# Down-projection weights of a SwiGLU stage: lower parts made by an accumulating DMA in place of VectorE

## The chip, the cores and the metric

The kernel runs on one core of a Trainium2 chip. The metric is the time of one execution on the device in microseconds (us); the lower, the better. The engines are named as the profile names them: PE is TensorE's matmul side and PEld its weight load, DVE is VectorE, ACT is ScalarE, POOL is GpSimd, and SP is SyncE, whose queue issues most DMAs here ("SPq" in the profile).

## The reference, cut to what matters

Two layers work on 640 token rows (128 of a context, 512 of a latent) of 1024 features. Each layer is SwiGLU, mixer (a convolution with a gating unit in layer 0, attention in layer 1), SwiGLU, each with a norm, a modulation and a gated residual around it. So there are four SwiGLU stages, and the change lies in these alone:

```python
def swiglu(h, wg, wu, wd):
    return (jax.nn.silu(h @ wg) * (h @ wu)) @ wd
...
    xp = residual(xp, swiglu(pre(xp, mp, norm_w[l, 0], 0), *f1), mp, norm_w[l, 1], 0, 0.5)
    xs = residual(xs, swiglu(pre(xs, ms, norm_w[l, 0], 0), *f1), ms, norm_w[l, 1], 0, 0.5)
```

Here `wg` and `wu` are 1024 x 2816 and `wd` is 2816 x 1024, all float32.

## The kernel before

Every large product is made of three. Each operand `w` is held as an upper part `hi` (`w` rounded to float32r) and a lower part `lo = w - hi`, and `mm3` (L198) adds hi·hi, hi·lo and lo·hi in PSUM. So every weight tile that comes from DRAM is split: `wload` (L178) issues the load on SP's queue into a `raw` tile, has ACT copy it to `hi`, and has DVE subtract `hi` from `raw` into `lo`. There are three `raw` buffers and six buffers each for `hi` and `lo`. A `raw` buffer is free for the next load when the last of its readers is done.

TensorE, VectorE and ScalarE execute their instructions in the order in which the program writes them (class `InOrder`, L58), so a copy that waits for its load holds up all that ACT has behind it. SP issues its loads in order too.

`ffn` (L557) works through the 22 chunks of 128 hidden features in four parts, `PARTS = [(0, 5), (5, 10), (10, 16), (16, 22)]`. For each chunk it runs two units, on token columns 0 to 383 (GA) and 384 to 639 (GB): 48 products each, then SiLU on ACT, a multiplication on DVE and a split of the result. At the end of each of the first three parts follow the down-projections of that part, first for output features 0 to 511 (here called half 0), then for 512 to 1023 (half 1): five token tiles, each a group of 15 products (18 in the third part) with a moving operand of 512 columns, taken from `wd`, and added to y. The weights of a half come in three pieces by `wdown` (L591): each holds two chunks (512 KB), but the third piece of the first two parts holds one (256 KB). `wdown(0)` is written ahead of the last chunk's GA unit, `wdown(1)` after the first token tile of half 0. The pieces are called first, second and third below. The fourth part loads its weights otherwise (L601, L632) and is not touched.

In between, `background` (L265) runs the modulation of later stages: a 512 KB load into a `raw` buffer (`mod_chunk`, L495) and two long multiply-and-sum instructions on DVE for each.

Of the kernel before, what the change touches and what calls it, by code (L numbers as in the profile page):

```python
# [18 lines left out]
T = NT * P  # L19
# [9 lines left out]
# the features of an attention head: first halves of both rotated quarters' pairs, then the second halves  # L29
HALVES = np.arange(64).reshape(2, 2, 16).transpose(1, 0, 2).reshape(64)  # L30
PARTS = [(0, 5), (5, 10), (10, 16), (16, 22)]
# token columns: 0..127 context (cond 0), 128..639 latent (cond 1)
# [4 lines left out]
def weave(main, fill, every=3):  # L37
    """run main, with one of fill after each `every` of them, then the rest of fill"""
    fill = list(fill)
    for n, f in enumerate(main):  # L40
        f()
        if n % every == every - 1 and fill:
            fill.pop(0)()
    for f in fill:
        f()


def segs(lo, hi):
    """parts of a token range with one condition: (from, to, condition)"""
    out = []  # L50
    if lo < NP:
        out.append((lo, min(hi, NP), 0))
    if hi > NP:
        out.append((max(lo, NP), hi, 1))
    return out


class InOrder:  # L58
    """an engine whose instructions are issued in the order in which they are written"""
# [18 lines left out]
class Core:  # L78
    """the NeuronCore; tensor, vector and scalar engine in written order"""
# [7 lines left out]
class Builder:  # L87
# [23 lines left out]
    # Slots of a tag are handed out in the order in which their tiles are first written here. Upper and  # L111
    # lower parts come from different engines, so that they have tags of their own.
# [25 lines left out]
    def split(self, src, hi, lo):  # L138
        """src = hi + lo exactly, both with 12 significant bits."""
        self.nc.scalar.activation(out=hi, in_=src, func=AF.Copy)  # L140
        self.nc.vector.tensor_tensor(out=lo, in0=src, in1=hi.bitcast(F32), op=ALU.subtract)

    def table(self, func):
        """has the scalar engine load func's table ahead of its use"""
        self.nc.scalar.activation(out=self.sm(1, "table"), in_=self.ones[:, 0:1], func=func)

    def wload_ahead(self, dram, nblk, blk=P, pieces=1, small=False):
        """starts the load of weights [128, nblk * blk]; closures that split them, and the list of nblk (hi, lo)
        pairs, there after the first of the closures. small: by way of tiles of their own for the pieces"""
# [33 lines left out]

    def fetch(self, key, dram, nblk, blk=P):
        """wload ahead of its use; take() returns it"""
# [3 lines left out]
    def fetch_ahead(self, key, dram, nblk, blk=P):  # L189
        """fetch() with the split left to the two closures that are returned: upper part, lower part"""  # L190
# [7 lines left out]
    def mm3(self, out, w, x, first, last):  # L198
        """out += w^T x with both operands in two parts"""
# [5 lines left out]
    def proj(self, w, h, g):  # L205
        """PSUM [128, n] = w^T h for one 128-wide output chunk, tokens g"""
# [6 lines left out]
    def proj2(self, ws, h, g, inserts=None):  # L213
        """two projections together, feature chunk by feature chunk; inserts: {k: emitted before chunk k}"""
# [9 lines left out]
    def proj_tok(self, ps, h, w, t):  # L224
        """ps [128 tokens of tile t, n] = h^T w"""
# [5 lines left out]
    def rsqrt_ops(self, ssq, scale, engine=None):  # L231
        """1/sqrt(ssq * scale + eps) on a few columns: the result and the instructions. engine: of the iterations"""
# [3 lines left out]
        # v holds -1/2 of the argument, the first guess comes from its bits  # L236
# [34 lines left out]
    def hi_lo(self, src, mods, c, lo, h):  # L271
        """h[c] columns from lo = src * G + shift, split: what makes the upper part and what then makes the lower
        one are to be called"""
# [11 lines left out]
    def turn(self, tiles, c):  # L285
        """PSUM [128 features of chunk c, tokens] from the normalised x"""
# [5 lines left out]
    def tail(self, last, nxt, fetches):  # L292
        """last(t): (closures for the last products of the sub-layer for token tile t, [closures that add the two
        halves to y]). Norms, residual and the next sub-layer's input h follow. What is left of h is in four
        dictionaries: closures to be called before the feature chunks of the next sub-layer's first three units on
        GA and of its first on GB. fetches: closures that start the loads of the next sub-layer's first weights
        and return the two closures that split them."""
# [6 lines left out]
        def sq(t, what, s=None):  # L304
            # sum of squares of x or y
# [13 lines left out]
        def both(tx, ty):  # L319
            # the columns of x[tx] and y[ty] together  # L320
# [64 lines left out]
        # the last tile: what follows its products goes between those of the next sub-layer's first three units  # L385
# [9 lines left out]
        def step(tiles=None, c=None):  # L395
            # transposes of a chunk; upper and lower parts of the one before
# [72 lines left out]
    def last_tail(self, last):  # L469
        """as tail(), for the last sub-layer"""  # L470
# [34 lines left out]
    def mod_final(self, l, slot, what):  # L505
        """what: 0 shift and scale, 1 gate"""
# [16 lines left out]
    def gate_rows(self, l, slot):  # L523
        """gg as rows along the features, the same on every partition"""
# [24 lines left out]
    def glu(self, pg, pu, out, g):  # L549
        """out (hi, lo) columns g = silu(pg) * pu"""  # L550
# [6 lines left out]
    def ffn(self, l, i, h, lead, nxt, fetches, started=None):  # L557
# [29 lines left out]
        for pi, (j0, j1) in enumerate(PARTS):  # L587
# [3 lines left out]
            def wdown(half):  # L591
                return [p for j in range(j0, j1, 2) for m in [min(2, j1 - j)]
                        for p in self.wload(a["wd"][l, i, j:j + m, :, half * 512:half * 512 + 512]
                                            .rearrange("j p m -> p j m"), m, 512)]
# [42 lines left out]
    def last_products(self, xs, ws, xsel=lambda x, t: tuple(u[:, t * P:(t + 1) * P] for u in x)):  # L637
        """for tail(): y[t] += sum over k of xs[k]^T ws[k]"""
# [21 lines left out]
    def conv_gmlp(self, h, lead, nxt, fetches):  # L660
# [46 lines left out]
        def shifted(c):  # L707
            # 32 channels x 4 shifts on the partitions, for the convolution on the tensor engine
# [5 lines left out]
            for q in range(4):  # L714
                nc.gpsimd.memset(sa[q], 0.0)
                for s in range(4):
                    # column j holds position j + s - HALF
# [61 lines left out]
        def mix(c, copy=lambda out, x: nc.scalar.activation(out=out, in_=x, func=AF.Copy)):  # L779
            # position mixing; what follows the products is returned as closures  # L780
# [72 lines left out]
        # LayerNorm over the conv channels, then swish  # L853
# [38 lines left out]
        for n, f in enumerate(parts):  # L892
# [3 lines left out]
            if n == 3:  # L896
                # from here on the products overwrite the normalised channels
# [9 lines left out]
    def first_products(self, dram, xs, xsel=lambda x, t: tuple(u[:, t * P:(t + 1) * P] for u in x), **kw):  # L907
        """y[t] = the first two of the products of an output projection: a function that starts
        the load of one half of the weights (closures that split them), and closures of the products"""
# [19 lines left out]
    def rope(self, s, pos, on_act=False):  # L929
        """s [128, ..]: latent columns, in place, at positions pos; a feature's partner lies 32 partitions off.  # L930
        Closures, and the last of them"""
# [6 lines left out]
        # the sines have the sign that they need with the partner  # L938
# [7 lines left out]
    def attention(self, h, lead, nxt, fetches):  # L946
# [4 lines left out]
        # keys of chunk 8 + n: latent tiles 1 and 2, cached ones, latent tiles 3 and 4, so that those of any window  # L951
        # lie side by side; the prompt's
# [29 lines left out]
        def rope(s, pos, on_act=False):  # L982
            """closures; the sum of each is left until the products of the next"""
# [25 lines left out]
        # upper parts of the keys of one head on both halves of the partitions, lower parts on their own  # L1009
# [48 lines left out]
        # values, tokens on partitions  # L1058
# [7 lines left out]
        def v_tile(t):  # L1066
            """closures: the values of tile t"""
# [8 lines left out]
        # chunk i holds head 8*(i//4) + i%4 in its lower and head 8*(i//4) + 4 + i%4 in its upper half  # L1076
# [3 lines left out]
        def window(t):  # L1080
            """columns of the keys, columns of the mask, values"""
# [6 lines left out]
        def prepare(t, engine=None):  # L1088
            """closures: both parts of the queries of tile t one above the other, upper parts where they were"""
# [554 lines left out]
```

## Time and profile before

| what | value |
|---|---|
| median of 2 runs | 2372.54 us (2371.78 and 2373.3) |
| the profiled execution, first to last instruction (span) | 2369.2 us |
| what lies between the span and the median | 3.3 us |
| DVE busy | 1354.3 us |
| ACT busy | 833.5 us |
| POOL busy | 111.4 us |
| DMA, mean over the span | 108 GB/s |

No time other than the span is given for the profiled execution itself. A profile row names line, engine, operation and tiles ("out<-in"), then the number of such instructions, their busy time and the mean duration of one in ns, and the idle time of the engine just ahead of them with what ended it. Most instructions stand under L68, the helper that records them in order, so groups are told apart by tiles and shapes. DVE's subtraction that makes the lower part of a weight is `w<-raw,w`, ACT's copy that makes the upper part is `w<-raw`. In a timeline row the first number is the start in us from the span's begin, the second the length.

### The profile page before, as it was taken

How to read it: one execution, taken by the hardware profiler on the slowest of the kernel's cores; microseconds unless marked ns; L12 is line 12 of the kernel's file. 1: busy time of each engine (PE TensorE's matmuls, PEld its weight loads, DVE VectorE, ACT ScalarE, POOL GpSimd, SP SyncE). 2: the span in 40 equal slices, each digit the busy share in tenths (PEclk: the TensorE clock that was granted, in tenths of full speed). 3: DMA queues.
4: the chain of work that ended last, by engine and by line, in shares of the span. 5: the costliest groups of instructions: out<-in, count | busy, mean ns of one | idle time of the engine just before them, and what ended most of it. 6: DMA issues, size and time to landing. Idle time of an engine off the chain costs nothing.

```text
span 2369.2 us, 35411 instructions
## 1 busy us (share of the span) xinstructions
PE 2343.9 (99%) x14484; PEld 2147.5 (91%) x14484; DVE 1354.3 (57%) x2419; ACT 833.5 (35%) x1507; POOL 111.4 (5%) x191
## 2 busy tenths in 40 slices
PE   9999999999999999999999999999899999999998
PEld 7999999999789899989899999998866798989897
DVE  5556665668775566523755666656888652333235
ACT  5322222363354221213532212225468553212122
POOL 1000000021100000000100000002220010000000
PEclk9999999999999999999999999999999999999999
DMA  7343444413223444422224444352000222222221
GB/s 290 117 141 134 152 136 163 137 56 101 73 86 98 134 159 131 147 87 90 67 89 139 151 142 160 134 171 75 28 21 17 92 76 85 72 81 81 80 73 70
DMA packets 85026, 256.82 MB, mean 108 GB/s; under 512 B 9824, under 2 KB 11744, under 8 KB 84096
## 3 DMA queue, kind: packets, MB, share of 16 engines
q1 hardware_dynamic: 83984, 252.74, 32.0%
q8 instruction: 113, 1.85, 0.3%
q0 software_dynamic: 880, 1.83, 0.2%
q14 instruction: 49, 0.40, 0.1%
HBM read 248.97 MB, written 2.93 MB: 106 GB/s over the span
## 4 chain that ended last, share of the span: by engine, by line
PE 94%; DVE 3%; POOL 1%; ACT 1%; issue 1%; DMA 1%; SPq 0%; DVEq 0%; POOLq 0%; ACTq 0%
PE ps L68 94%; DVE tmp L68 1%; DVE w L68 1%; DVE Y L68 1%; POOL nwq L68 1%; DVE act L68 0%; DMA X<-x 0%; DVE X L68 0%; DMA act<-wmod 0%; POOL nwy L68 0%; ACT w L68 0%; ACT Y L68 0%; DVE nwy L68 0%; DVE nwq L68 0%; ACT act L68 0%
## 5 line engine op out<-in xcount | busy, mean ns | idle before, releaser
L68 PE MATMUL ps<-act,w 128*128 128x384 f32 (+4 forms) x9984 | 1479.5, 314 | 8.2 <-DVE w L68 6.8
L68 PEld LDWEIGHTS ps<-act,w 128*128 128x128 f32 (+2 forms) x9984 | 1425.0, 186 | 32.8 <-issue 15.8
L68 PE MATMUL ps<-w,act 128*128 128x512 f32 (+1 forms) x3480 | 782.9, 384 | 3.1 <-ACT tmp L68 3.1
L68 PEld LDWEIGHTS ps<-w,act 128*128 128x128 f32 x3480 | 627.4, 189 | 136.3 <-ACT tmp L68 3.5
L68 DVE TENSOR_TENSOR w<-raw,w 128x1024 fp32r<-128x1024 f32 (+1 forms) x313 | 365.1, 1199 | 151.4 <-ACT w L68 149.9
L68 ACT ACTIVATE w<-raw 128x1024 fp32r<-128x1024 f32 (+1 forms) x313 | 315.5, 1030 | 367.5 <-PE ps L68 146.9
L68 DVE CUSTOM_DVE_ANT_0 scr<-raw,cbc 128x1024 bf16<-128x1024 f32 x256 | 312.9, 1222 | 12.0 <-DMA raw<-wmodT 6.9
L68 DVE TENSOR_TENSOR tmp<-tmp,ps 128x384 f32<-128x384 f32 (+1 forms) x176 | 85.7, 487 | 401.2 <-ACT tmp L68 357.1
L68 ACT ACTIVATE tmp<-ps 128x384 f32<-128x384 f32 (+2 forms) x198 | 83.7, 425 | 652.4 <-PE ps L68 652.0
L68 DVE TENSOR_TENSOR act<-tmp,act 128x256 fp32r<-128x256 f32 (+2 forms) x306 | 135.3, 448 | 133.7 <-ACT act L68 132.5
L68 DVE TENSOR_TENSOR Y<-Y,ps 128x512 f32<-128x512 f32 x140 | 95.6, 686 | 192.9 <-PE ps L68 192.7
L68 ACT ACTIVATE act<-tmp 128x256 fp32r<-128x256 f32 (+3 forms) x304 | 128.3, 433 | 124.1 <-DVE tmp L68 123.9
L68 ACT ACTIVATE Y<-ps 128x512 f32<-128x512 f32 (+2 forms) x96 | 50.8, 532 | 147.6 <-PE ps L68 147.1
L68 ACT ACTIVATE tmp<-ps,sh,G 128x256 f32<-128x256 f32 (+1 forms) x120 | 60.3, 525 | 22.7 <-PE ps L68 22.7
L68 ACT ACTIVATE tmp<-Y 128x1024 bf16<-128x1024 f32 (+2 forms) x39 | 35.1, 901 | 71.4 <-DVE Y L68 71.4
L68 DVE SCALAR_TENSOR_TENSOR act<-act,cw,act 128x640 f32<-128x640 f32 (+14 forms) x60 | 54.5, 909 | 1.8
L68 ACT ACTIVATE Y<-X 128x1024 f32<-128x1024 f32 x30 | 31.8, 1059 | 54.3 <-DVE X L68 50.7
L68 PE MATMUL ps<-ident,Y 128*128 128x128 f32 x260 | 46.7, 273 | 2.6 <-DVE Y L68 2.2
L68 DVE CUSTOM_DVE_ANT_0 raw<-ps,ggrow 128x384 f32<-128x384 f32 (+1 forms) x64 | 41.1, 680 | 12.8 <-PE ps L68 11.4
L68 POOL TENSOR_TENSOR nwq<-nwy 128x1 f32<-128x1 f32 (+1 forms) x30 | 17.9, 595 | 613.2 <-DVE nwy L68 611.7
L68 PEld LDWEIGHTS ps<-ident,Y 128*128 128x128 f32 x260 | 34.4, 140 | 11.7 <-DVE Y L68 3.9
L68 ACT ACTIVATE raw<-raw,nmx 128x384 f32<-128x384 f32 (+1 forms) x64 | 42.2, 669 | 1.0 <-DVE nmx L68 0.9
(149 smaller groups left out, 758.6 us busy)
## 6 DMA issues: line engine op xcount, KB each, us to landing
raw<-wmodT SPq DMA_DIRECT2D x128, 512.0 KB, 3.8
raw<-wg SPq DMA_DIRECT2D x88, 512.0 KB, 4.5
raw<-wu SPq DMA_DIRECT2D x88, 512.0 KB, 3.6
raw<-wd SPq DMA_DIRECT2D x80, 512.0 KB, 4.0
act<-wmod SPq DMA_DIRECT2D x24, 256.0 KB, 6.5
ggrow<-grow SPq DMA_DIRECT2D x6, 1024.0 KB, 4.6
raw<-win SPq DMA_DIRECT2D x12, 512.0 KB, 3.7
raw<-wqkv SPq DMA_DIRECT2D x10, 512.0 KB, 3.8
```

The source lines that it names most:

```text
L68: i = method(*args, **kw)
```

## The change

`wdown` calls a new function, `wload_added`, in place of `wload`, for all pieces of the first three parts of each stage. ACT first writes the negated upper part into the `lo` tile (a copy with scale -1), then the upper part into `hi`. Then a DMA on POOL's queue loads the same weights a second time from DRAM and adds them onto `lo`, so that it holds `w - hi`. DVE's subtraction of these pieces is gone. There are 3 pieces x 2 halves x 3 parts x 4 stages = 72 of them. The rest of the diff removes comments, so that later lines have other numbers.

```diff
+    def wload_added(self, dram, nblk, blk):
+
+        n = nblk * blk
+        raw = self.raw(n)
+        cut = lambda u: u.rearrange("p (a b) -> p a b", a=nblk)
+        self.nc.sync.dma_start(out=cut(raw), in_=dram)
+        hi, lo = self.wpair(n)
+        self.nc.scalar.activation(out=lo, in_=raw, func=AF.Copy, scale=-1.0)
+        self.nc.scalar.activation(out=hi, in_=raw, func=AF.Copy)
+        self.nc.gpsimd.dma_start(out=cut(lo), in_=dram, accum_op=ALU.add)
+        return [(hi[:, b * blk:(b + 1) * blk], lo[:, b * blk:(b + 1) * blk]) for b in range(nblk)]
...
             def wdown(half):
                 return [p for j in range(j0, j1, 2) for m in [min(2, j1 - j)]
-                        for p in self.wload(a["wd"][l, i, j:j + m, :, half * 512:half * 512 + 512]
-                                            .rearrange("j p m -> p j m"), m, 512)]
+                        for p in self.wload_added(a["wd"][l, i, j:j + m, :, half * 512:half * 512 + 512]
+                                                  .rearrange("j p m -> p j m"), m, 512)]
```

On ACT, at the first part of the first stage, half 0, these rows stood before (`raw_1060`, `raw_1066` and `raw_1072` are the three pieces as loaded, `ps_1080` is the result of the GA unit that runs meanwhile; a name in brackets after "waits" is a semaphore, DMAHW of a load on SP's queue):

```order
L68 ACTIVATE act_936<-tmp_1049 128x256 [waits DVE_49]
L68 ACTIVATE w_1062<-raw_1060 128x1024 [waits DMAHW5_49]
L68 ACTIVATE w_1068<-raw_1066 128x1024 [waits DMAHW6_49]
L68 ACTIVATE w_1074<-raw_1072 128x512 [waits DMAHW7_49,Activation_49]
L68 ACTIVATE tmp_1130<-ps_1080 128x384 [waits PE_49]
```

In the changed kernel ACT's rows at the same place are these (`raw_1060`, `raw_1067` and `raw_1074` are the pieces, `w_1063`, `w_1070` and `w_1077` their lower tiles):

```order
L68 ACTIVATE act_936<-tmp_1049 128x256 [waits DVE_49]
L68 ACTIVATE w_1063<-raw_1060 128x1024 [waits DMAHW5_49]
L68 ACTIVATE w_1062<-raw_1060 128x1024
L68 ACTIVATE w_1070<-raw_1067 128x1024 [waits DMAHW6_49]
L68 ACTIVATE w_1069<-raw_1067 128x1024
L68 ACTIVATE w_1077<-raw_1074 128x512 [waits DMAHW7_49]
L68 ACTIVATE w_1076<-raw_1074 128x512 [waits Activation_49]
L68 ACTIVATE tmp_1133<-ps_1083 128x384 [waits PE_49]
```

Each piece has two copies on ACT where it had one, the negated one first, and the SiLU of the unit stands behind six copies where it stood behind three.

On POOL's queue the accumulating DMAs follow each other, with the last of the DMAs that set up the convolution ahead of them (DMASW is a semaphore of a DMA on POOL's queue):

```order
L1479 DMA slnb<-slnb 128x4 [waits DMASW2_49]
L193 DMA w_1063<-wd 128x2x512 [waits DVE_49,DMASW3_49,PE_49,Activation_49]
L193 DMA w_1070<-wd 128x2x512 [waits DVE_49,DMASW4_49,PE_49,Activation_49]
L193 DMA w_1077<-wd 128x512 [waits DVE_49,DMASW5_49,PE_49,Activation_49]
L193 DMA w_1225<-wd 128x2x512 [waits DVE_49,DMASW6_49,PE_49,Activation_49]
L193 DMA w_1232<-wd 128x2x512 [waits DVE_49,DMASW7_49,PE_49,Activation_49]
L193 DMA w_1239<-wd 128x512 [waits DVE_49,DMASW0_49,PE_49,Activation_49]
```

All 18 of a stage stand together in this way: no other instruction of POOL stands between those of one stage.

On PE, at the start of the same half 0, the second product and the eighth are the first that need the lower parts of the first and the second piece:

```order
L68 MATMUL ps_1205<-w_1062,act_706 128x512 [waits Activation_49]
L68 MATMUL ps_1205<-w_1063,act_706 128x512 [waits DMASW3_49]
L68 MATMUL ps_1205<-w_1062,act_707 128x512
L68 MATMUL ps_1205<-w_1062,act_708 128x512
L68 MATMUL ps_1205<-w_1063,act_708 128x512
L68 MATMUL ps_1205<-w_1062,act_709 128x512
L68 MATMUL ps_1205<-w_1069,act_800 128x512 [waits Activation_49]
L68 MATMUL ps_1205<-w_1070,act_800 128x512 [waits DMASW4_49]
```

PE's order is as before, but these two products wait for a DMA on POOL's queue where they waited for DVE.

On SP the order of the loads is the same; what they wait for is not, since the `raw` buffers are handed out otherwise. Before:

```order
L159 DMA raw_1060<-wd 128x2x512 [waits DMAHW5_49,DMAHW2_49,DVE_49]
L159 DMA raw_1066<-wd 128x2x512 [waits DMAHW3_49,DVE_49]
L159 DMA raw_1072<-wd 128x512 [waits DMAHW4_49,DVE_49]
L498 DMA raw_1135<-wmodT 128x1024 [waits DMAHW5_49,DVE_49]
L498 DMA raw_1196<-wmodT 128x1024 [waits DMAHW6_49,DVE_49]
```

And now:

```order
L189 DMA raw_1060<-wd 128x2x512 [waits DMAHW5_49,DMAHW2_49,DVE_49]
L189 DMA raw_1067<-wd 128x2x512 [waits DMAHW3_49,DVE_49]
L189 DMA raw_1074<-wd 128x512 [waits DMAHW5_49,Activation_49]
L510 DMA raw_1138<-wmodT 128x1024 [waits DMAHW4_49,DVE_49]
L510 DMA raw_1199<-wmodT 128x1024 [waits DMAHW6_49,Activation_49]
```

The third piece (`raw_1074`) takes the buffer of the first piece as soon as ACT has read it twice; before, it took the buffer of a modulation chunk that DVE had to finish.

## The prediction

> **What bounds the kernel now.** I read the page first: the span, the engines' shares and the chain that ended last.
>
> ```profile
> span 2369.2 us, 35411 instructions
> PE 2343.9 (99%) x14484; PEld 2147.5 (91%) x14484; DVE 1354.3 (57%) x2419; ACT 833.5 (35%) x1507; POOL 111.4 (5%) x191
> ...
> PE 94%; DVE 3%; POOL 1%; ACT 1%; issue 1%; DMA 1%; SPq 0%; DVEq 0%; POOLq 0%; ACTq 0%
> ```
>
> PE is idle for 2369.2 - 2343.9 = 25.3 us, and 94% of the chain is PE. That would not do alone, since matmuls overlap and busy rows can hide a slow pace; so the view by windows over four stretches comes next (the columns are PE, PEld, DVE, ACT and POOL busy, then the granted clock, the DMA share and GB/s): three down-projections, then the stretch of attention.
>
> ```profile
> 105.00:139.50 34.50, 34.50 (x151) 27.94 (x150) 18.67 (x29) 10.11 (x15) 0.00 (x0) 1.00 0.43 145
> 329.40:371.10 41.70, 41.70 (x183) 33.96 (x182) 19.97 (x30) 6.98 (x8) 0.00 (x0) 1.00 0.35 114
> 1969.50:2004.50 35.00, 35.00 (x153) 28.37 (x153) 6.17 (x7) 10.47 (x16) 0.00 (x0) 1.00 0.22 75
> ...
> 1600.00:1800.00 200.00, 188.08 (x1187) 157.93 (x1186) 155.53 (x342) 121.61 (x297) 42.06 (x56) 0.97 0.11 37
> ```
>
> In a down-projection PE has no gap and the full clock, and 34.5 us for 150 products is 0.23 us each. The third row is the test that matters: DVE is busy 6.17 us of 35 there against 18.67 in the first, and PE's pace is the same. About half of PE's idle time, 11.9 us, lies in the stretch of attention. The waits of PE, longest first, and one row of the timeline tell the same:
>
> ```profile
> PE ps L68 <- DVE w L68: 6.8, 2, 6.6
> ...
> 1715.47 0.47 PE L68 MATMUL ps<-act,w 128*128 128x128 f32 x1 [6.57 <-DVE w L68]
> ```
>
> The whole of PE's waiting for DVE's `w` is one wait in attention, whose `w` are query parts and not weights. So DVE's subtraction of down-projection weights delays nothing now.
>
> **The change, part by part.** What goes and what comes is priced by two rows of the view by groups, shapes kept apart:
>
> ```profile
> L68 ACT ACTIVATE w<-raw 128x1024 fp32r<-128x1024 f32 x297 | 305.9, 1052 | 335.9 <-PE ps L68 143.2 <-DMA raw<-wu 76.1 <-DMA raw<-wd 41.1
> ...
> L68 DVE TENSOR_TENSOR w<-raw,w 128x1024 fp32r<-128x1024 f32 x297 | 354.6, 1226 | 144.3 <-ACT w L68 142.8 <-PE ps L68 1.0
> ```
>
> DVE loses 56 subtractions of 1.23 us (512 KB) and 16 of 0.69 us (256 KB, row below), 80 us in all. None of it is on PE's path, so its worth is 0; with all of PE's 25.3 idle us it could not be more than 1.1%. ACT gains 56 copies of 1.05 us and 16 of 0.63 us, 69 us, and goes to some 900 us of 2369: hidden in itself, but the copies move ACT's order, see below. A copy with a scale is taken at the price of the plain one. POOL gains 72 DMA issues:
>
> ```profile
> L1510 POOL DMA_DIRECT2D ggrow<-mask x1 | 0.6, 561 | 0.0
> ```
>
> At 0.56 us each these are 40 us on an engine that is busy for 111, and nothing else of POOL stands between those of one stage, so no Newton step or memset waits behind them.
>
> What decides is when the accumulating DMA has landed and when PE wants its result. First part of the first stage, timeline:
>
> ```profile
> 91.67 2.23 ACT L68 ACTIVATE w<-raw 128x1024 fp32r<-128x1024 f32 x2
> ...
> 97.33 0.63 ACT L68 ACTIVATE w<-raw 128x512 fp32r<-128x512 f32 x1 [3.43 <-DMA raw<-wd]
> 98.00 0.69 DVE L68 TENSOR_TENSOR w<-raw,w 128x512 fp32r<-128x512 f32 x1 [1.09 <-ACT w L68]
> ...
> 104.68 25.68 PE L68 MATMUL ps<-w,act 128*128 128x512 f32 x110
> ...
> 108.84 2.00 ACT L68 ACTIVATE w<-raw 128x1024 fp32r<-128x1024 f32 x2
> ...
> 111.38 0.63 ACT L68 ACTIVATE w<-raw 128x512 fp32r<-128x512 f32 x1 [0.55 <-DMA raw<-wd]
> ```
>
> Half 0 starts at 104.68. Its second product wants the first piece's lower part (104.9), the 8th the second's (106.3), the 14th the third's (107.7). Today all three are there at 98.7, nine us early. Now ACT negates the first piece at 91.67 to 92.72, copies it until 93.77, negates the second until 94.8 and the third, at the latest, until 97.96. That leaves an accumulating DMA 12.2, 11.5 and 9.7 us from its release to PE's need. In half 1, which starts 75 products later at 122.1, the negated copies end at 109.9, 112.0 and 113.7 and the needs are 122.3, 123.7 and 125.1: 12.4, 11.7 and 11.4 us.
>
> The third part has three full pieces and is the tightest:
>
> ```profile
> 307.58 12.20 SPq L159 DMA_DIRECT2D raw<-wd  x3
> ...
> 316.42 1.04 ACT L68 ACTIVATE w<-raw 128x1024 fp32r<-128x1024 f32 x1
> ...
> 317.75 1.06 ACT L68 ACTIVATE w<-raw 128x1024 fp32r<-128x1024 f32 x1 [0.29 <-DMA raw<-wd]
> ...
> 323.18 1.06 ACT L68 ACTIVATE w<-raw 128x1024 fp32r<-128x1024 f32 x1 [4.36 <-DMA raw<-wd]
> ...
> 329.42 41.70 PE L68 MATMUL ps<-w,act 128*128 128x512 f32 x180
> ...
> 330.52 1.04 ACT L68 ACTIVATE w<-raw 128x1024 fp32r<-128x1024 f32 x1
> ```
>
> 41.70 us for 180 products is 0.232 us each. The needs are 329.7, 331.0 and 332.4; the negated copies end at 317.5, 319.6 and 324.2: 12.2, 11.5 and 8.2 us. The last is a lower bound: the third load was issued at 319.4 (the end of the x3 row) and landed 3.8 us later, and it now takes the first piece's buffer, which ACT leaves at 318.5, so about 9 us are left. The SiLU of the unit is then behind six copies and starts near 324.4 to 325.3 where the third copy ended at 324.2; its result is wanted after 15 products of the first tile, at 332.9: hidden. In half 1 (start 350.3) the margins are over 15 us.
>
> Now the DMA. No row of this trace shows an accumulating one. The nearest:
>
> ```profile
> raw<-wd SPq DMA_DIRECT2D x80, 512.0 KB, 4.0
> ...
> raw<-wd SPq DMA_DIRECT2D x16, 256.0 KB, 2.6
> ...
> ggrow<-mask POOLq DMA_DIRECT2D x1, 384.0 KB, 5.0
> ...
> ggrow<-rsin POOLq DMA_DIRECT2D x1, 256.0 KB, 2.9
> ...
> GB/s 290 117 141 134 152 136 163 137 56 101 73 86 98 134 159 131 147 87 90 67 89 139 151 142 160 134 171 75 28 21 17 92 76 85 72 81 81 80 73 70
> ```
>
> From 256 to 512 KB a load grows by 1.4 us, so 512 KB is 1.2 us fixed and 2.8 us of moving; POOL's queue adds 0.3 (2.9 against 2.6). The new DMA reads the weights and also the tile it adds to: twice the bytes read, and I take the moving twice: 1.5 + 5.6 = 7.1 us for 512 KB and 4.3 for 256 KB. The low end is a plain load by POOL, 4.3 us; for the high end I take four times the moving (both reads, the sum and the write one after the other and none overlapped), 12.7 us. I take 7.1 since the load's row is of the same bytes on the same engines. The three of a half can also queue behind each other: their spacing S lies between 5.6 (nothing of two DMAs overlaps) and 3.6 (twice 512 KB at the 290 GB/s that the first slice kept up).
>
> Lateness of the third piece (0 where negative), L being the landing time of 512 KB: half 0 of the first two parts (8 halves) L + 1.5 S - 15.0; half 0 of the third part (4) L + 2 S - 15.0; half 1 of the first part (4) L + 1.5 S - 15.2; the others have 3 to 6 us more. With L = 7.1 and S = 3.6 all are negative: 0. With S = 5.6 they are 0.5, 3.3 and 0.3: 8 x 0.5 + 4 x 3.3 + 4 x 0.3 = 18 us. I take S near 3.6, for the slice held its rate for 59 us. Sum: 0 for DVE, 0 for ACT, 0 for POOL, 0 to 18 for PE's new wait; taken at the low end, the span stays 2369 and the time, 3.3 us above it as in the median of 2372.5, is 2373, with 2369 to 2391 as this case's own range.
>
> The Trainium skill, page "Collectives: The Full Stack", section "The bandwidth ceiling: the fold count and why AG ≠ RS ≠ AR", has a reason for the factor: an add in the DMA path costs its second source read rather than the arithmetic, and it measured 32.35 against 62.28 GB/s for a copy. No run here shows this yet; by that rule the high end of four times would not come about, and the sum would be the one above.
>
> **The rivals.** *Slower: the accumulating DMA becomes PE's wait.* Nothing in the rows excludes a DMA that adds at a third or a quarter of a load's rate, and POOL's queue has an odd row (384 KB in 5.0 us). With L = 1.5 + S the three latenesses reach 47 us in sum (2%) at S = 6.3: 8 x 2.3 + 4 x 5.4 + 4 x 2.1 = 48. That is where it decides. At three times the moving, S = 8.4 and L = 9.9, they are 7.5, 11.7 and 7.3, and the other halves (margins 18.3 and 21.6) 4.2 and 5.1: 60 + 47 + 29 + 17 + 20 = 173, or 2546 us; at four times some 2720. Against it: the margins of 8 to 12 us are two to three plain loads.
>
> *A little slower: the second read takes bandwidth from the loads.* While the first two pieces accumulate, the third is being loaded, then two modulation chunks; the first stages already use a DMA share of 0.35 to 0.43. If one load's moving (512 KB at 290 GB/s, 1.8 us) comes ahead of the accumulating DMAs on the engines, L is 8.9, and with S = 5.6 the latenesses are 2.3, 5.1 and 2.1: 8 x 2.3 + 4 x 5.1 + 4 x 2.1 = 47 us; in the last stage, where no modulation runs (share 0.22), they stay at the 18 / 4 from above, so 0.75 x 47 + 4.5 = 40. The case covers 19 to 47 us, 2391 to 2419. In the Trainium skill, page "DMA: Bandwidth & Descriptors", section "Queues, rings and completion order", each DMA engine takes turns between the queues it has work for, packet by packet, so that a load and an accumulation would each get about half. By that rule this rival holds whenever they meet; no run here shows it.
>
> *Faster: DVE's 80 us come off PE's time.* It would need PE to wait for DVE in these stages; the rows above show no such wait. All of PE's idle time gone gives 2347, still within 2%.
>
> **How the numbers follow.** A change of 2%, 47 us, is about what a measurement of this kernel can tell from none. Likeliest, no wait or up to 18 us: 0.74, predicted time 2373. A little slower, 2391 to 2419: 0.08. Slower by more: 0.16. Faster by more: 0.02. Same is 0.74 + 0.08 = 0.82. The range must hold 8 in 10: from 2366, some us under the likeliest's own 2369 for what runs differ by, to 2415, most of the second case: about 0.81.
>
> **What would show it.** The accumulating DMAs' rows: near 7 us to landing for 512 KB; PE's waits without a row for a DMA into `w`; DVE busy near 1275 us, ACT near 900. Wrong would be PE rows with a gap ahead of the 2nd, 8th or 14th product of a half, longest in the third part: then L or S is mis-sized, and the gap's length says by how much.

## The result, and the profile after

The changed kernel takes 2397.74 us (median of 2 runs, 2396.99 and 2398.49) against 2372.54 before: a ratio of 1.0108, 95% interval 1.0078 to 1.0137. That is 25.2 us more, 1.1%: within the 2% that the prediction calls the same, inside its range of 2366 to 2415, and 24.7 us above the time it named. The size and the place are those of its second case, not of the likeliest one. Of all the executions reported here, two of one kernel ("tile held, in order" in the table below) took 3842 and 6631 us, for no reason that a run shows; its median is that of all nine, its ratio that of the other seven.

The page of the changed kernel, the span, the engines and three groups (instructions, then busy us and mean ns, then idle us ahead of them and what ended most of it):

```profile
span 2396.7 us, 35578 instructions
...
PE 2357.0 (98%) x14484; PEld 2151.6 (90%) x14484; DVE 1280.0 (53%) x2347; ACT 893.1 (37%) x1579; POOL 193.4 (8%) x263
...
L68 PE MATMUL ps<-w,act 128*128 128x512 f32 (+1 forms) x3480 | 794.1, 387 | 17.9 <-DMA w<-wd 14.5
...
L193 POOL DMA_DIRECT2D w<-wd x72 | 81.9, 1140 | 1143.1 <-ACT w L68 1014.7
...
raw<-wd SPq DMA_DIRECT2D x80, 512.0 KB, 4.6
w<-wd POOLq DMA_DIRECT2D x56, 512.0 KB, 10.3
```

VectorE and ScalarE stand where the diff puts them: 74 us less, 60 us more. POOL pays 1.14 us for an issue. The down-projection's products now wait 14.5 us for the adding DMA, which lands 10.3 us after its issue. The waits of PE, which had no such row before (total us, times, longest):

```profile
PEld ps L68 <- DMA w<-wd: 24.7, 24, 2.8
...
PE ps L68 <- DMA w<-wd: 14.5, 17, 2.3
```

Where the time went is read by taking the same PE instruction in both traces, half by half, and asking how much later it starts. Half 0 of the third part loses 4.6, 4.6, 5.7 and 1.3 us in the four down-projections, 16.2 in sum. Half 0 of the first part loses 3.1 in all four, of the second 1.8, half 1 of the first part 4.5, of the second 0.3. These are 25.9 of the 27.5 us between the two profiled spans. Outside the down-projections little is lost: some tenths in attention, and 1.4 us at the start of the program, where some executions run at half the clock for 3.4 us and others do not, with and without adding DMAs.

The tightest place, half 0 of the third part in the first down-projection, in the timeline after (start, length, engine):

```profile
321.63 3.89 ACT L68 ACTIVATE w<-raw 128x1024 fp32r<-128x1024 f32 x4
322.96 1.20 POOL L193 DMA_DIRECT2D w<-wd  x1 [97.77 <-ACT w L68]
323.65 0.37 SPq L189 DMA_DIRECT2D raw<-wd  x1
324.61 1.32 SPq L510 DMA_DIRECT2D raw<-wmodT  x2
324.86 1.20 POOL L193 DMA_DIRECT2D w<-wd  x1 [0.69 <-DVE mf L68]
328.21 2.01 ACT L68 ACTIVATE w<-raw 128x1024 fp32r<-128x1024 f32 x2 [2.69 <-DMA raw<-wd]
329.56 1.19 POOL L193 DMA_DIRECT2D w<-wd  x1 [3.51 <-ACT w L68]
...
334.64 1.78 PE L68 MATMUL ps<-w,act 128*128 128x512 f32 x7
336.62 1.66 PE L68 MATMUL ps<-w,act 128*128 128x512 f32 x6 [0.20 <-DMA w<-wd]
340.59 4.60 PE L68 MATMUL ps<-w,act 128*128 128x512 f32 x12 [2.31 <-DMA w<-wd]
```

The three issues stand at 322.96, 324.86 and 329.56. PE does seven products, waits 0.20 us for the second piece, does six more and waits 2.31 us for the third, which landed 11.0 us after its issue. The third load and a modulation load start between the first and the second issue, a second modulation load 0.7 us after the second. What the 16 DMA engines did from the first issue to the third landing, 17.6 us (digits: tenths busy in 40 slices; queue: packets, MB, share of the 16 engines' time; q0 holds POOL's DMAs, q1 the loads):

```profile
DMA  0009315799999999999999999999999999999999
...
q0 software_dynamic: 816, 1.57, 48.9%
q1 hardware_dynamic: 1061, 2.56, 44.4%
```

From 3.5 us after the first issue every slice is 90% busy or more. 1.57 MB of additions take 0.489 x 17.6 = 8.6 us of all engines, 5.5 us per MB; 2.56 MB of loads take 7.8 us, 3.0 per MB. An addition costs 1.8 times a load here, and while it is under way the loads take nearly as much of the engines as it does. The factor is not a constant: read in the same way in the runs below, from the first issue to the third landing of this half, it is 2.2 or 2.3 (added from the loaded tile; tile held, in order) and 2.5 (added from the tile in rows of 2 KB). The Trainium skill, page "Collectives: The Full Stack", section "The bandwidth ceiling: the fold count and why AG ≠ RS ≠ AR", has two source reads for an add and measured a factor of 1.93. The 1.8 to 2.5 of these runs lie on both sides of it.

The rest of the loss there is the clock (the view by windows: us, busy time of the engines, granted clock, DMA share, GB/s; the three rows are the end of the wait, the 3.5 us after it and what follows):

```profile
335.00:341.20 6.20, 3.69 (x16) 2.38 (x15) 3.17 (x6) 2.29 (x3) 0.53 (x1) 1.00 1.00 261
341.20:344.70 3.50, 3.50 (x10) 2.71 (x9) 0.69 (x1) 2.13 (x3) 1.86 (x2) 0.51 0.56 102
344.70:350.00 5.30, 5.30 (x24) 4.30 (x24) 0.69 (x1) 0.67 (x1) 0.00 (x0) 1.00 1.08 267
```

Behind the wait the clock is 0.51 for 3.5 us: ten products in 3.5 us, where the row below has 24 in 5.3. That costs about 1.7 us more (half of 3.4). The same follows the waits of 2.3 us in the second and third down-projection.

### The profile page after: what moved, and what is told of

Its sections match the earlier page's. It is cut to its first block, busy times and chain, and to the rows that moved or that the text cites. A ratio compares the mean times of both kernels' runs of the same rounds, so it can differ in the third digit from the quotient of the medians.

```text
span 2396.7 us, 35578 instructions
## 1 busy us (share of the span) xinstructions
PE 2357.0 (98%) x14484; PEld 2151.6 (90%) x14484; DVE 1280.0 (53%) x2347; ACT 893.1 (37%) x1579; POOL 193.4 (8%) x263
## 5 line engine op out<-in xcount | busy, mean ns | idle before, releaser
L68 PE MATMUL ps<-w,act 128*128 128x512 f32 (+1 forms) x3480 | 794.1, 387 | 17.9 <-DMA w<-wd 14.5
L68 PEld LDWEIGHTS ps<-w,act 128*128 128x128 f32 x3480 | 629.4, 190 | 160.4 <-DMA w<-wd 24.7
L68 ACT ACTIVATE w<-raw 128x1024 fp32r<-128x1024 f32 (+1 forms) x385 | 375.4, 1014 | 348.0 <-PE ps L68 123.3
L68 DVE TENSOR_TENSOR w<-raw,w 128x1024 fp32r<-128x1024 f32 x241 | 288.4, 1227 | 129.4 <-ACT w L68 128.1
L193 POOL DMA_DIRECT2D w<-wd x72 | 81.9, 1140 | 1143.1 <-ACT w L68 1014.7
## 6 DMA issues: line engine op xcount, KB each, us to landing
w<-wd POOLq DMA_DIRECT2D x56, 512.0 KB, 10.3
```

What stands on the lines that cost most here:

```text
L68: i = method(*args, **kw)
L193: self.nc.gpsimd.dma_start(out=cut(lo), in_=dram, accum_op=ALU.add)
```

## Experiments

The theory after this reading: the adding DMA is too late because it shares busy DMA engines with the loads; VectorE's and ScalarE's changed work plays no part. The rivals: the adding DMA is slow by itself (a lag before its first packet, its rows, its second read), or ScalarE's second copy delays something. Each run is compared with runs of the kernel before on the same chip, median some 2372 us; "lost" is the ratio less 1, in us.

| kernel | median us | ratio (95%) | lost us | 512 KB to landing, median us |
|---|---|---|---|---|
| changed kernel | 2397.74 | 1.0108 (1.0078 to 1.0137) | 25 | 10.3 |
| plain loads in place of the additions | 2373.01 | 1.0003 (0.9993 to 1.0012) | 1 | 6.4 |
| ScalarE's copies alone | 2371.97 | 0.9999 (0.9989 to 1.0008) | 0 | none |
| third piece by VectorE | 2378.0 | 1.0025 (1.0015 to 1.0035) | 6 | 10.1 |
| rows of 4 KB | 2379.23 | 1.0028 (1.0016 to 1.0039) | 7 | 8.9 |
| modulation loads cut | 2378.86 | 1.0027 (1.0018 to 1.0037) | 6 | 8.8 |
| 4 of 72 pieces by VectorE | 2384.35 | 1.0054 (1.0037 to 1.0071) | 13 | 10.2 |
| half 0 alone | 2389.03 | 1.0071 (1.0056 to 1.0086) | 17 | 10.4 |
| added from the loaded tile | 2371.92 | 1.0000 (0.9991 to 1.0009) | 0 | 5.5 |
| the same, rows of 2 KB | 2375.69 | 1.0017 (1.0007 to 1.0027) | 4 | 6.1 |
| additions cut in two | 2393.7 | 1.0091 (1.0076 to 1.0106) | 22 | 8.9 (256 KB) |
| tile held, not in order | 2391.83 | 1.0086 (1.0068 to 1.0104) | 20 | 10.3 |
| tile held, in order | 2377.62 | 1.0023 (1.0011 to 1.0034) | 5 | 6.6 |

**Plain loads in place of the additions.** The same DMAs without the addition, so that the lower part is the weight itself.

```diff
-        self.nc.gpsimd.dma_start(out=cut(lo), in_=dram, accum_op=ALU.add)
+        self.nc.gpsimd.dma_start(out=cut(lo), in_=dram)
```

> The added DMA stays where it is, on the same queue and with the same waits, but only loads the weights into the lower tile and does not add (so the products with the lower parts are wrong: the addition is left out). In the changed kernel the first of three such DMAs lands some 8.3 us after its issue, of which some 4 us pass before its first packet, and the next ones 4 to 5 us later each. Theory 'the second read of the addition costs it': landing near 4.5 to 5.5 us for 512 KB and a spacing near 2 to 3 us, no wait of PE for these DMAs, time 2371 to 2376 us. Rival 'POOL's queue costs it whether it adds or not (making the descriptors, the two rows of 2 KB a partition)': landing 8 us, spacing 4 us or more, PE's waits and the time stay near 2390 to 2398 us.

No time is lost, and no wait of PE for these DMAs is left. The issue shows in the page's group:

```profile
L193 POOL DMA_DIRECT2D w<-wd x72 | 48.7, 677 | 1157.1 <-ACT w L68 1108.7
...
w<-wd POOLq DMA_DIRECT2D x56, 512.0 KB, 6.4
```

0.68 us an issue against 1.14, and 6.4 us to landing, longer than expected: these too share the engines with the loads, the first of a half landing 4.3 us after its issue (median) and the second 6.6 to 9.8. The extra bytes from HBM and POOL's queue cost nothing here, with the same loads beside them; it takes the addition to lose time.

**ScalarE's copies alone.** Negated copy and plain copy as in the changed kernel, the lower part again by VectorE.

```diff
-        self.nc.gpsimd.dma_start(out=cut(lo), in_=dram, accum_op=ALU.add)
+        self.nc.vector.tensor_tensor(out=lo, in0=raw, in1=hi.bitcast(F32), op=ALU.subtract)
```

> ACT makes both copies of each piece as in the changed kernel, but VectorE's subtraction then writes the lower part and no DMA adds. Theory 'PE waits for the DMA alone': 2371 to 2375 us, no wait of PE in the down-projections. Rival 'the six copies ahead of the SiLU delay ACT and so PE': a part of the 25 us stays, 2380 us or more.

Nothing is lost: the 60 us of ScalarE and the load that starts a copy later are free, and that rival falls.

**Third piece of each half by VectorE.**

```diff
-                        for p in self.wload_added(a["wd"][l, i, j:j + m, :, half * 512:half * 512 + 512]
+                        for p in (self.wload_added if j < j0 + 4 else self.wload)(a["wd"][l, i, j:j + m, :, half * 512:half * 512 + 512]
```

> The third piece of each half (24 of the 72) goes back to ACT's copy and VectorE's subtraction; the first two of each half still go by the accumulating DMA. Theory 'it is the third in the queue that is late': in half 0 of the third part the second piece lands within 0.5 us of PE's need, so nearly nothing is lost, 2372 to 2378 us. Rival 'each accumulating DMA costs PE by itself (contention, the clock, waits of the first piece)': two thirds of the 25 us stay, 2385 to 2392 us.

5.7 us are left of 25. The two additions that remain still take 10.1 us to landing, but the third need, the late one, is met.

**Rows of 4 KB.** The addition takes as many bytes from other weights that lie in rows of 4 KB, so 128 rows in place of 256.

```diff
-        self.nc.gpsimd.dma_start(out=cut(lo), in_=dram, accum_op=ALU.add)
+        k = self.added = getattr(self, "added", -1) + 1
+        long = self.a["wg"][k // 36, k // 18 % 2, k % 18]
+        self.nc.gpsimd.dma_start(out=lo, in_=long[:, :n], accum_op=ALU.add)
```

> The accumulating DMA adds as many bytes, but takes them from rows of 4 KB that lie together (gate weights, so the products with the lower parts are wrong), 128 rows in place of 256. If the number of rows sets the time to the first packet (descriptors made by POOL) it falls from 4 us to 2 to 3 us and POOL's issue from 1.2 to some 0.6 us; PE's waits shrink to under 8 us and the time is 2375 to 2385 us. If the bytes set it, landing (8.3 us) and spacing (4 to 5 us) stay and the time is 2392 to 2400 us.

About a quarter of the loss is left, as expected. The issue is 0.88 us, and the first packet follows the issue by 1.6 us in place of 2.7 to 4.5. I read this at first as the price of the number of rows, a lag of the queue; the additions cut in two, below, start as early and gain almost nothing. What this run changes besides is the size of a packet. The trace has an addition of 512 KB as 256 packets of 2 KB in the changed kernel and as 128 of 4 KB here; a modulation load has packets of 4 KB in both. In the same half, over 18.1 us that hold its three additions, POOL's queue shows:

```profile
q0 software_dynamic: 432, 1.57, 47.6%
```

The engine time of the additions is the same, 0.476 x 18.1 = 8.6 us, 5.5 per MB, and the modulation loads still start 1.7 us behind the first issue. But the first addition lands after 6.3 us in place of 9.0, and the third load beside it takes 6.7 us in place of 4.5: the additions get a larger share of the same engines. That this comes from the larger packets agrees with turns that are taken packet by packet, but no run here changes the size of the packets alone.

**Modulation loads cut.**

```diff
-        nc.sync.dma_start(out=raw, in_=self.a["wmodT"][l, ch])
+        nc.sync.dma_start(out=raw[:, 0:16], in_=self.a["wmodT"][l, ch, :, 0:16])
+        raw = self.cbc[:, 0, :]
```

> The loads of the modulation weights are cut to 16 of 1024 columns (8 KB instead of 512 KB each) and VectorE takes its sums from a tile that is there anyway, so that its work is the same and the modulation, and with it all output, is left wrong. The buffers keep their order. Theory A, the adding DMAs are slowed by the loads that run beside them: then the third part's half 0 of the first three down-projections loses what it loses in the last one, which has no such loads (1.3 us instead of 4.6, 4.6 and 5.7, so 11 us less), the first parts lose 1 to 3 us less, the median to landing falls from 10.3 us to 8 to 9, and the time is 2383 to 2387 us. Theory B, it is their own pace and the loads do not matter: 2395 to 2399 us, landing 10 us or more.

Theory A holds, and by more than it gave: 6.5 us lost, and the first addition of most halves in the first three down-projections lands 5.8 to 6.3 us after its issue, where it was 6.8 to 9.6. These three lose 3.6 us in sum in place of 24. The last one, which had no such loads, stays late: 8.1 to 9.4 us to landing. The edit does more than it was meant to: with the modulation loads gone the buffers come free sooner, and in the third part of the first down-projection the third load goes out at 309.38, 10.2 us ahead of the first addition, where it stood 0.7 us behind it. So the first addition starts with neither the third load nor a full modulation load beside it, and the third piece is ready earlier. How much of the gain is the modulation loads' alone, this run does not tell.

**Four of 72 pieces by VectorE**, the third of half 0 of the third part.

```diff
-                        for p in self.wload_added(a["wd"][l, i, j:j + m, :, half * 512:half * 512 + 512]
+                        for p in (self.wload if pi == 2 and half == 0 and j == j0 + 4 else self.wload_added)(a["wd"][l, i, j:j + m, :, half * 512:half * 512 + 512]
```

> Only the third 512 KB piece of half 0 of the third part, 4 of the 72 adding DMAs, goes back to VectorE. Theory, the loss is the lateness of the third in the queue, stage by stage: the trace puts 4.6, 4.6, 5.7 and 1.3 us on these four halves, of which the second piece has some tenths, so 2381 to 2384 us, and no stretch of 3.4 us at the half clock after these places. Rival, a price per adding DMA (25 us over 72): 2396 us.

Four of 72 pieces take off 12 us; by their number alone it would be 1.4. The median is just above what was expected, the profiled execution (2381.43 us) in it, and no half clock follows these places. The loss is lateness at one need, not a price per DMA.

**Half 0 alone.**

```diff
-                        for p in self.wload_added(a["wd"][l, i, j:j + m, :, half * 512:half * 512 + 512]
+                        for p in (self.wload if half else self.wload_added)(a["wd"][l, i, j:j + m, :, half * 512:half * 512 + 512]
```

> Half 1 of each part goes back to VectorE, half 0 keeps its 36 adding DMAs. Theory, each half loses for itself: half 0 lost 16.2 us in the third parts, 3.1 in the first and 1.8 in the second, half 1 lost 4.5, so 2392 to 2395 us. Rival, the queue carries lateness from one half to the next, so that half 1's DMAs hold up what comes after them: then more than half 1's 4.5 us comes off, below 2390 us.

2389.0 is 3 us below the theory's range, and by the numbers set down the rival won. The trace says otherwise. The waits of half 0 are those of the changed kernel: 2.27, 2.29 and 2.37 us in the third parts, where it has 2.31, 2.29 and 2.31. But here the clock does not fall behind them, three times 1.7 us; 21.1 less 5.1 is the 16 us that this trace shows for half 0. It is not the profiled execution alone: the granted clock is 0.995 in all four of this kernel, 0.993 and 0.994 in the changed kernel's two. Half 1 took its share as read, and no lateness is handed on.

**Added from the loaded tile**, the one that ScalarE copies from, in place of HBM.

```diff
-        self.nc.gpsimd.dma_start(out=cut(lo), in_=dram, accum_op=ALU.add)
+        self.nc.gpsimd.dma_start(out=lo, in_=raw, accum_op=ALU.add)
```

> The adding DMA reads the loaded tile (4 KB rows, 128 of them) instead of the weights in HBM a second time. The tile is then held until it has landed, some 7 us longer, and the third load, which takes the first piece's buffer, starts that much later. Theory, the number of rows sets the lag and where they come from does not matter: first packet 1.6 us after the issue, landing about 6.5 us after it, but the third piece is then as late as now or later: 2396 to 2412 us. Rival, the second read of HBM is what costs: landing 5 us or less, and below 2385 us.

The theory missed. The rival's time holds and its landing nearly does (5.1 us for the first of a half, 5.5 over all), but the loss is gone whole, and the place that is read from need not be the reason. My theory had the third load wait for the first piece's tile. The timeline shows what happens:

```profile
317.61 0.87 POOL L193 DMA_DIRECT2D w<-raw  x1 [97.67 <-ACT w L68]
319.27 0.37 SPq L189 DMA_DIRECT2D raw<-wd  x1
319.51 0.87 POOL L193 DMA_DIRECT2D w<-raw  x1 [1.02 <-DVE mf L68]
322.88 4.84 SPq L510 DMA_DIRECT2D raw<-wmodT  x2
326.12 0.87 POOL L193 DMA_DIRECT2D w<-raw  x1 [5.75 <-ACT w L68]
...
329.28 7.09 PE L68 MATMUL ps<-w,act 128*128 128x512 f32 x30
```

The third load goes out at 319.27, 0.2 us ahead of the second addition, and PE runs on without a gap. It is the modulation loads that wait for the held tile: they start at 322.88, 5.3 us after the first addition's issue, where the changed kernel has them 1.7 us after it. So this edit does two things at once, another place to read from, and loads held back.

**The same, rows of 2 KB**: the loaded tile has a gap of 64 bytes after each 2 KB.

```diff
-        raw = self.raw(n)
-        self.nc.sync.dma_start(out=cut(raw), in_=dram)
+        raw = cut(self.raw(n + 16 * nblk))[:, :, :blk]
+        self.nc.sync.dma_start(out=raw, in_=dram)
...
-        self.nc.gpsimd.dma_start(out=cut(lo), in_=dram, accum_op=ALU.add)
+        self.nc.gpsimd.dma_start(out=cut(lo), in_=raw, accum_op=ALU.add)
```

> As the run that adds from the loaded tile, but the tile has a gap of 64 bytes after each 2 KB, so that the adding DMA moves 256 rows of 2 KB per 512 KB as in the changed kernel. It tells the number of rows from the place that they are read from. If the rows cost it: the first packet 3 to 4 us after the issue as in the changed kernel, landing near 8 us, and 2382 to 2392 us. If the second read of HBM costs it: landing 5 to 6.5 us, and 2371 to 2376 us. Between the two, each has a share.

Between the two, near the lower: landing 6.1 us in place of 5.5, 1.14 us an issue in place of 0.87, and 3.9 us lost in place of none. So the rows have a share, and a small one where the loads are held back. The first packet comes 1.8 us after the issue with 256 rows, so that the 2.7 to 4.5 us of the changed kernel are no price of the rows alone.

**Additions cut in two**, 128 rows each, from HBM.

```diff
-        self.nc.gpsimd.dma_start(out=cut(lo), in_=dram, accum_op=ALU.add)
+        for b in range(nblk):
+            self.nc.gpsimd.dma_start(out=cut(lo)[:, b], in_=dram[:, b], accum_op=ALU.add)
```

> Each adding DMA of 512 KB is cut into two of 128 rows of 2 KB, each from HBM as in the changed kernel; the bytes and the rows are the same in sum. If the lag before the first packet goes with the rows of one DMA (1.6 us at 128, 2.8 to 4.5 at 256): the first 256 KB is under way some 2 us earlier, all three of a half land that much earlier, and the time is 2377 to 2386 us; POOL pays two issues of 0.9 us for one of 1.2. If the lag is one of the queue, or the pace of moving alone decides: 2393 to 2402 us.

The first packet comes 1.6 us after the issue, as the lag theory said, and it is worth almost nothing: the first 512 KB is through 8.8 us after the first issue in the third part of the first down-projection, where one DMA took 9.0, and the time is the rival's. What an early start gains, the pace takes back: the packets are of 2 KB as before, and the engines are shared all the same.

**Tile held**, adding from HBM: does holding back the loads do it, or the place to read from? A DMA of 64 bytes from the tile behind each addition.

```diff
         self.nc.gpsimd.dma_start(out=cut(lo), in_=dram, accum_op=ALU.add)
+        self.nc.gpsimd.dma_start(out=self.sm(16, "hold")[0:1], in_=raw[0:1, 0:16])
```

> The changed kernel, adding from HBM, with a 64-byte DMA from the loaded tile put behind each adding DMA in POOL's queue, so that the tile is held until the addition is through, as it is where the addition reads the tile. The modulation loads that take these tiles then start after the first addition instead of beside it. It tells the two effects of adding from the tile apart. If holding the loads back is what helps: the first 512 KB lands some 6 us after its issue instead of 9 in the first three stages, and the time is 2376 to 2384 us, as without modulation loads. If where the second operand is read from is what helps: landing stays at 8 to 9 us, and 2390 to 2402 us.

Inconclusive: the small DMA went out ahead of the addition, and held nothing. Its 2391.83 are another run with the modulation loads beside the additions. The next one keeps both in order.

```diff
-        self.nc.gpsimd.dma_start(out=cut(lo), in_=dram, accum_op=ALU.add)
+        q = InOrder(self.tc, self.nc.gpsimd)
+        q.dma_start(out=cut(lo), in_=dram, accum_op=ALU.add)
+        q.dma_start(out=self.sm(16, "hold")[0:1], in_=raw[0:1, 0:16])
```

> In the last run the 64-byte DMA went ahead of the adding one, since only the loaded tile released it, and the modulation loads ran beside the addition as before. Now the two are kept in their written order, so that the tile is held until the small DMA behind the addition is through. If holding the loads back is what helps when the addition reads the tile: the first 512 KB lands some 6 us after its issue in the first three stages, and 2374 to 2384 us. If where the second operand is read from is what helps: landing stays at 8 to 9 us there, and 2388 to 2402 us. In the last stage, without modulation loads, both expect what the changed kernel has, 8 to 9 us.

Holding the loads back is most of it: 4.9 us lost, with the second read still from HBM and 256 rows. The same place in its timeline, and the queues from the first issue to the third landing, 16.9 us:

```profile
317.33 1.24 POOL L68 DMA_DIRECT2D w<-wd  x1 [95.89 <-ACT w L68]
...
318.98 0.37 SPq L189 DMA_DIRECT2D raw<-wd  x1
319.23 1.22 POOL L68 DMA_DIRECT2D w<-wd  x1
...
324.86 4.38 SPq L512 DMA_DIRECT2D raw<-wmodT  x2
327.55 1.22 POOL L68 DMA_DIRECT2D w<-wd  x1 [6.56 <-ACT w L68]
...
329.00 3.17 PE L68 MATMUL ps<-w,act 128*128 128x512 f32 x13
334.25 3.97 PE L68 MATMUL ps<-w,act 128*128 128x512 f32 x16 [2.08 <-DMA w<-wd]
```

```profile
q0 software_dynamic: 909, 1.57, 58.5%
q1 hardware_dynamic: 540, 1.52, 25.1%
```

1.52 MB of loads stand beside the additions, where there were 2.56. The two modulation loads are in both, but they now start 7.5 and 11.6 us after the first addition's issue in place of 1.7 and 2.6; the two that are gone are weights of half 1, which stood behind them and now start only after the third landing. The first 512 KB lands 6.0 us after its issue (median over the halves; 8.5 in the changed kernel), its first packet 2.0 us after it. In the last down-projection, where I expected no help, it lands after 5.8 to 6.2 us too: there the loads held back are those of weights.

Not all of the gain is earlier landing. The trace has three waits of PE left, ahead of the 14th product in the third parts: 2.08, 1.43 and 1.53 us, where the changed kernel has 2.31, 2.29 and 2.31. The third load, beside two additions, now takes 7.1 us in place of 4.5, so that the third addition goes out 1.5 us ahead of the half's start in place of 5.1. But the half clock does not follow these waits, which is 5.1 us of the 20 won. The other 15 are the smaller waits, which are gone altogether: those at the 8th product, those in the first and second parts, and the last down-projection's.

What reading from the tile adds to this is the step from 6.0 to 5.3 us (2 KB rows in both), and from 4.9 to 3.9 us lost, whose intervals overlap; with 4 KB rows the rest goes as well.

No version here beats the kernel before. PE is busy for 99% of its span, so all that a change to this step can do is not be waited for; adding from the loaded tile does that, with VectorE 74 us less busy at the same time.

## Why the prediction came out as it did

- **Right by its second case**: the time lies in the range because the range was drawn to hold most of that case. The case that gave 2373 did not occur.
- **DVE, ACT and POOL at 0**: right. (PE's waiting for DVE's `w` before, taken for one wait, is two, of 6.57 and 0.25 us, both in attention; that changes nothing.) The copies alone and the plain loads lose nothing; the busy times are within 7 us of those forecast (1280 for 1275, 893 for 900). A POOL issue was priced at 0.56 us and costs 1.14, on an engine that has nothing else to do there.
- **The needs and margins**: right. The timeline after has 13.0 us from the first copy to the half's start (329.42 - 316.42 before, 334.64 - 321.63 after), the third load goes out once ScalarE has left the first piece's tile, and the waits stand where the prediction looked: ahead of the 8th and 14th product, longest in the third part.
- **L = 7.1 us and S near 3.6, "for the slice held its rate for 59 us"**: this step failed. As prices of an addition by itself they are good and even high: with the loads held back the first lands 6.0 us after its issue, 6.3 from the negated copy, and the next 3.3 us later. But they were used as if it were by itself. Beside the loads the first takes 8.5 us from the issue (8.8 from the copy) and the second 5.0 more. A rate that the engines keep is one that they share; the two shares, of loads and additions, should have been added: in the 17.6 us of the tightest half they are 7.8 and 8.6 us of all engines.
- **"The first stages already use a DMA share of 0.35 to 0.43"**: a mean over 35 to 42 us, taken as slack. The modulation and weight loads come in bursts at just the place where the additions run, and there the share is 1.0 (335.00 to 341.20 in the changed kernel).
- **The second case, "a little slower"**: its mechanism and its range, 2391 to 2419, are what happened, and 0.08 was too little for it. It had L = 8.9 and S = 5.6 and 40 us. Its third part is near (18.6 forecast, 16.2 measured), in part by luck: 5.1 of the 16.2 are the clock, which the forecast did not have. Near is also half 1 of the first part (0.75 x 4 x 2.1 + 0.3 = 6.6 against 4.5); half 0 of the first two parts is not (0.75 x 18.4 + 1 = 14.8 against 4.9), since the third piece, of 256 KB there, lands 5.0 + 2.1 = 7.1 us after the first (medians over the halves) and not 1.5 x 5.6 = 8.4. The last down-projection lost 1.8 us, where a fourth of the sum without contention was 4.5.
- **The rule of turns** of the Trainium skill, page "DMA: Bandwidth & Descriptors", section "Queues, rings and completion order", by which this case would hold whenever the two meet: the runs agree. Loads moved away from the additions are worth 19 us (modulation loads cut) and 20 us (tile held, in order), and larger packets of the additions beside the same loads 18 us (rows of 4 KB).
- **The clock** was not priced: three waits of 2.3 us cost another 1.7 us each.
- **Slower by over 2% and faster**: an addition is 1.8 to 2.5 times a load in engine time, not three or four times, and the decision point S = 6.3 was not reached: the second addition lands 5.0 us after the first. Nothing was gained from VectorE's 74 us.

## What to carry to other kernels

Before a transfer is moved to the DMA queues, take the engines' busy share in the few microseconds between its release and its need, not the mean over the stage, and add to its own time that of every load that starts in this window. Where a late transfer is the trouble, look first at what can be started behind it: holding loads back until the addition was through, by a DMA of 64 bytes, took away four fifths of the loss here, a quarter of that by a clock that did not fall. Rows of 4 KB in place of 2 took away nearly three quarters without holding anything back. Reading the operand from the tile that lies on the chip lost nothing in rows of 4 KB; in rows of 2 KB the gain over HBM is not clear of the noise. There the tile that its reader holds orders the loads behind it at no cost, since they had slack.

## What the runs showed of the hardware

- Adding DMAs of 512 KB cost 5.5 us of all 16 engines per MB, loads 3.0, in the same 17.6 us; in three runs with the loads held back additions cost 5.9 to 6.6 and loads 2.6 to 2.8. POOL's issue of one takes 1.2 us for 256 rows and 0.88 for 128, against 0.7 for a plain DMA of 256 rows.
- The first packet of an adding DMA from HBM of 256 rows came 2.0 us after its issue with the loads held back and 2.7 to 4.5 us with loads beside it. With loads beside it, it came after 1.6 us where the DMA had 128 rows and after 1.4 where it had 256 and did not add. So it takes rows, loads and addition together; why is open.
- A wait of 2.3 us can be followed by 3.4 us at half clock or by none. In the profiled execution of the changed kernel it was three of three, in that of half 0 alone none of three with nearly the same waits at the same places. Elsewhere a wait of 2.07 us was followed by it (rows of 4 KB) and one of 2.08 was not (tile held, in order). The Trainium skill, page "TensorE: Matmul & The Clock Gate", section "Part 1: The HAM clock gate (the "warmup" mystery)", has a window of some 3.4 us that runs free of the program. The length of 3.4 us agrees; that a gap's cost depends on where the window stands would fit, and is not shown. The Trainium skill, the same page, section "HAM oscillation — how this bites in real kernels", asks for no gaps over some 3.4 us; the three here were shorter and cost all the same.
